# Down projection of one hybrid layer: five groups of eight full products, or two groups of seven half-size forms

## The chip, the core and the metric

The kernel runs on one NeuronCore of one Trainium2 chip. The core has five engines with a queue of their own each: TensorE (PE, with its weight load shown apart as PEld), VectorE (DVE), ScalarE (ACT), GpSimd (POOL) and SyncE (SP), which issues all DMA transfers here. The metric is the device time of one execution in microseconds; the value for a kernel is the median of its runs.

## The reference, cut to what matters

One layer: modulated normalisation, short convolution and bidirectional mLSTM side by side, output projection, then a feed-forward block with a 3-tap convolution between its two projections, and a last normalisation. There are T = 2176 tokens (128 of a prompt, 2048 of a sample), D = 1024 channels and D_FF = 2816 = 22 x 128. All products are in fp32.

```
up = (h2 @ w_up)                          # (T, 2 * D_FF)
up = conv3(up, conv_ffn_w, conv_ffn_b, axis=ffn_axis)
a, gg = jnp.split(up, 2, axis=-1)
x = x + gate2 * ((jax.nn.silu(gg) * a) @ w_down)
...
y_prompt = rmsnorm(xp, final_norm)
y_sample = rmsnorm(xs, final_norm)
```

The change concerns `u @ w_down` with u = silu(gg) * a, that is 2176 x 2816 times 2816 x 1024, and the residual and the normalisation that follow.

## The kernel before, in words

Everything lies in one function, `hymba_kernel`, with channels on the 128 partitions and tokens along the rows. An fp32 product is made of three products in a rounded format: a factor is split into a high half (rounded by ScalarE) and a low half (what is left, by a subtraction), and high x high, high x low and low x high are summed in PSUM. So each operand that TensorE reads has passed ScalarE once and VectorE or GpSimd once.

The kernel has four stages:

1. Phase 0 and 1 (to L543 and on): modulation (`mod_dve`, L505-518), projections of the heads, short convolution, mLSTM, output projection. A generator `side` (L536) is advanced by the loops over the heads and the short convolution; each of its steps adds work that is not of the loop itself: the modulation's rows are multiplied on VectorE from tiles `wm`, five of them in rotation.
2. The up projection (L890-978): already in seven products of half size, in an order `ORDER` that is written out. For each of 22 tiles j of the feed-forward width, its results `raw` go through the convolution `conv` (L893-923: taps on VectorE at L900, ScalarE at L906 and L920, the product at L921), and u is stored to a DRAM tile `uD`.
3. The down projection (L981-1075). Tokens are cut into five groups (L981). For a group, all 22 slices of u are loaded and split (`load_u`, high half L999, low half L1000). For each of eight output blocks m, the 22 x 128 columns of weights are loaded in two halves of 1408 columns, split on ScalarE (L1011), GpSimd and VectorE (L1013, 704 columns each); then 22 x 3 products (L1044-1046) run into one PSUM accumulator `d`. There are four such accumulators. `close` (L1048-1058) takes it out of PSUM with gate and residual in one VectorE operation (L1051) and adds its squares to `ss`. The last product block of the last group is cut at 256 tokens.
4. The last normalisation, `finish` (L1017-1025): PE sums the squares over partitions (`inv_rms`, L124), VectorE and GpSimd make the inverse root (L127, L128), PE spreads it over all partitions (`spread`, L135), VectorE scales the eight blocks (L1024), and each is stored. It is called after the first block of the next group, and at the very end.

The framework puts each engine's instructions into a fixed order beforehand, from the order of the code, and each engine runs its queue in that order; a transfer waits in SP's queue until its buffer is free. The weights of the next block and the u of the next group are asked for in the code ahead of the products that run meanwhile (`nw`, `nus`).

Of the kernel before, what the change touches and what calls it, by code (L numbers as in the profile page):

```python
# [10 lines left out]
F32 = mybir.dt.float32  # L11
# [15 lines left out]
FT = 22  # L27
EPS = 1e-6
# [27 lines left out]
def hymba_kernel(ctx: ExitStack, tc: tile.TileContext, I, O):  # L56
# [17 lines left out]
    uD = dr.tile([FT, P, T], F32, name="uD")  # L74

# [235 lines left out]
    with ExitStack() as ph1:  # L311
# [151 lines left out]
        with tc.tile_pool(name="start", bufs=1, side="right") as stp:  # L463
# [70 lines left out]

            late()
            side = chain(first_stats(), mod_dve())  # L536
# [353 lines left out]
    with ph2:  # L890
        up = ctx.enter_context(tc.tile_pool(name="up", bufs=1))
# [89 lines left out]
    GR = [(0, 436), (436, 436), (872, 436), (1308, 434), (1742, 434)]  # L981
    NG = 436
    with ExitStack() as ph3:
        dq = ph3.enter_context(tc.tile_pool(name="dq", bufs=2, side="right"))
        du = ph3.enter_context(tc.tile_pool(name="du", bufs=8, side="right"))
        pools = {}
        for j0 in range(0, FT, 4):
            pool = ph3.enter_context(tc.tile_pool(name=f"du{j0}", bufs=1))
            for j in range(j0, min(j0 + 4, FT)):
                pools[j] = pool  # L990
        dp = ph3.enter_context(tc.tile_pool(name="dp", bufs=2))
        pd = ph3.enter_context(tc.tile_pool(name="pd", bufs=4, space=PSUM))

        def load_u(j, t0, n):
            f = du.tile([P, NG], F32, name="us")
            Q.dma_start(f[:, :n], uD[j][:, t0:t0 + n])
            uh = pools[j].tile([P, NG], F32R, name=f"uh{j}")
            ul = pools[j].tile([P, NG], F32R, name=f"ul{j}")
            S.activation(uh[:, :n], f[:, :n], AF.Copy)  # L999
            V.tensor_sub(ul[:, :n], f[:, :n], uh[:, :n].bitcast(F32))  # L1000
            return uh, ul

        def load_d(m):
            ws = []
            n = FT * P // 2
            for q in range(2):
                st = dq.tile([P, n], F32, name="st")
                Q.dma_start(st, I["w_down"][m][:, q * n:(q + 1) * n])
                wh = dq.tile([P, n], F32R, name="wh")
                wl = dq.tile([P, n], F32R, name="wl")  # L1010
                S.activation(wh, st, AF.Copy)  # L1011
                for e, a, b in ((G, 0, 704), (V, 704, n)):
                    e.tensor_sub(wl[:, a:b], st[:, a:b], wh[:, a:b].bitcast(F32))  # L1013
                ws.append((wh, wl))
            return ws
# [135 lines left out]
```

## Time and profile before

| | us |
|---|---|
| median of 3 runs | 2602.16 (2601.05 to 2602.48) |
| profiled execution | 2600.9 |
| its span, first to last instruction | 2599.1 |
| phases 0 and 1, to the first up product | about 1100 |
| up projection, to the end of its last product | about 949 |
| down projection, from there to the end of its last product | 539.5 |
| tail, from there to the last transfer | 10.5 |
| TensorE busy in the down projection (536.40 of 539.50) | 99% |

The page's first lines give busy time by engine, and its rows by line (`L1044 PE MATMUL d<-uh,wh`) give the tile written, the tiles read, the shape and the number of instructions. Rows of the timeline have the start in us from the span's beginning, the duration in us, and in brackets the idle time in front and what ended it. A row of the stage table has the stretch, then busy time and count of PE, PEld, DVE, ACT and POOL, the granted TensorE clock, the share of the DMA engines and GB/s. The granted clock over the whole span is 0.990. Rows of one line have minimum / median / maximum in ns, the first and last start, and the shapes. A row of transfers has the count, the KB of one and the us from issue to landing.

### The profile page before, as it was taken

The numbers are of one execution on the slowest core, as the hardware profiler recorded it, in microseconds if no ns is written. First come the engines' busy times: TensorE is split into PE (matmuls) and PEld (weight loads), VectorE is DVE, ScalarE is ACT, GpSimd is POOL, SyncE is SP. The second block draws the span as 40 slices with busy tenths as digits, with TensorE's granted clock in tenths as the row PEclk, the third lists the DMA queues.
The fourth block names the chain that finished last, engine by engine and source line by source line (L and its number), as shares of the span: only waits on it lengthen the run. The fifth ranks groups of instructions, "written<-read, shape, count | busy, mean of one in ns | idle before, by whom it ended". The sixth has DMA issues, their size and how long they took to land.

```text
span 2599.1 us, 40164 instructions
## 1 busy us (share of the span) xinstructions
PE 2520.1 (97%) x15121; PEld 2391.7 (92%) x15121; DVE 1519.6 (58%) x2495; ACT 1091.0 (42%) x1986; POOL 751.5 (29%) x545
## 2 busy tenths in 40 slices
PE   8999999999998989899999999999999999999998
PEld 7999999999998988899999998788888899999998
DVE  3993241223366556787686668867767735535353
ACT  4521152322355445464454446545555524424231
POOL 2442242211334343322121111221221233333332
PEclk9999999999999989999999999999999999999999
DMA  8783142565477877863243224222222647456362
GB/s 278 246 267 92 60 147 85 153 175 163 148 215 242 252 237 222 288 215 126 81 144 124 81 73 143 91 97 82 90 97 82 211 138 239 160 193 224 119 207 84
DMA packets 233380, 414.16 MB, mean 159 GB/s; under 512 B 21586, under 2 KB 173026, under 8 KB 231522
## 3 DMA queue, kind: packets, MB, share of 16 engines
q1 hardware_dynamic: 233186, 411.60, 48.7%
q8 instruction: 119, 1.95, 0.3%
q14 instruction: 75, 0.61, 0.1%
HBM read 316.57 MB, written 94.94 MB: 158 GB/s over the span
## 4 chain that ended last, share of the span: by engine, by line
PE 67%; DMA 6%; DVE 5%; issue 2%; ACT 1%; POOL 1%; SPq 0%; DVEq 0%; POOLq 0%; ACTq 0%
PE d L1044 7%; PE d L1045 7%; PE d L1046 7%; PE pa L955 6%; PE pa L957 6%; PE pa L956 6%; PE acc L203 3%; PE acc L201 3%; PE acc L202 3%; PE pb L955 3%; PE pb L957 3%; PE pb L956 3%; PE pc L956 2%; PE pc L955 2%; PE pc L957 2%
## 5 line engine op out<-in xcount | busy, mean ns | idle before, releaser
L201 PE MATMUL acc<-hH,wh 128*128 128x384 f32 (+1 forms) x1536 | 513.8, 335 | 7.4 <-DVE row L446 4.8
L203 PE MATMUL acc<-hH,wl 128*128 128x384 f32 (+1 forms) x1536 | 506.0, 329 | 0.0
L202 PE MATMUL acc<-hL,wh 128*128 128x384 f32 (+1 forms) x1536 | 505.4, 329 | 0.0
L291 POOL TENSOR_TENSOR wl<-st,wh 128x512 fp32r<-128x512 f32 x132 | 184.1, 1395 | 684.6 <-ACT wh L290 654.8
L110 POOL TENSOR_TENSOR wl<-wst,wh 128x512 fp32r<-128x512 f32 (+1 forms) x160 | 235.7, 1494 | 447.9 <-ACT wh L107 438.3
L955 PE MATMUL pa<-tH,wh 128*128 128x288 f32 (+1 forms) x1056 | 348.2, 330 | 5.8 <-DVE raw L969 3.8
L957 PE MATMUL pa<-tH,wl 128*128 128x288 f32 (+1 forms) x1056 | 346.2, 328 | 1.0 <-DVE wl L291 1.0
L956 PE MATMUL pa<-tL,wh 128*128 128x288 f32 (+1 forms) x1056 | 346.8, 329 | 0.0
L1044 PE MATMUL d<-uh,wh 128*128 128x436 f32 (+3 forms) x902 | 321.8, 357 | 2.4 <-ACT raw L967 2.4
L1045 PE MATMUL d<-ul,wh 128*128 128x436 f32 (+3 forms) x902 | 322.3, 357 | 0.0
L1046 PE MATMUL d<-uh,wl 128*128 128x436 f32 (+3 forms) x902 | 321.2, 356 | 0.0
L201 PEld LDWEIGHTS acc<-hH,wh 128*128 128x128 f32 x1536 | 291.6, 190 | 9.6 <-DVE row L446 5.6
L203 PEld LDWEIGHTS acc<-hH,wl 128*128 128x128 f32 x1536 | 291.4, 190 | 0.2 <-issue 0.2
L202 PEld LDWEIGHTS acc<-hL,wh 128*128 128x128 f32 x1536 | 291.5, 190 | 0.0
L1013 POOL TENSOR_TENSOR wl<-st,wh 128x704 fp32r<-128x704 f32 x80 | 191.1, 2389 | 341.3 <-ACT wh L1011 316.6
L1011 ACT ACTIVATE wh<-st 128x1408 fp32r<-128x1408 f32 x80 | 110.4, 1380 | 330.9 <-PE d L1045 309.5
L900 DVE SCALAR_TENSOR_TENSOR tt<-raw,fw,tt 128x127 f32<-128x127 f32 (+4 forms) x264 | 245.1, 949 | 3.5 <-ACT tt L906 2.5
L955 PEld LDWEIGHTS pa<-tH,wh 128*128 128x128 f32 x1056 | 198.3, 188 | 23.1 <-ACT c L962 2.6
L957 PEld LDWEIGHTS pa<-tH,wl 128*128 128x128 f32 x1056 | 199.0, 188 | 17.0 <-DVE wl L291 1.4
L956 PEld LDWEIGHTS pa<-tL,wh 128*128 128x128 f32 x1056 | 198.7, 188 | 15.5
L290 ACT ACTIVATE wh<-s 128x512 fp32r<-128x512 f32 x176 | 110.9, 630 | 177.0 <-PE pc L956 96.0
L1044 PEld LDWEIGHTS d<-uh,wh 128*128 128x128 f32 x902 | 170.3, 189 | 12.0 <-ACT raw L967 2.8
(215 smaller groups left out, 4892.5 us busy)
## 6 DMA issues: line engine op xcount, KB each, us to landing
st<-in_w_down SPq DMA_DIRECT2D x80, 704.0 KB, 4.1
st<-in_w_up SPq DMA_DIRECT2D x88, 512.0 KB, 4.8
wst<-in_w_in SPq DMA_DIRECT2D x48, 512.0 KB, 4.3
uD<-tt SPq DMA_DIRECT2D x44, 544.0 KB, 2.7
R<-nD SPq DMA_DIRECT2D x34, 512.0 KB, 6.3
wm<-in_w_modr SPq DMA_DIRECT2D x32, 512.0 KB, 4.7
us<-uD SPq DMA_DIRECT2D x66, 218.0 KB, 4.0
wst<-in_w_out SPq DMA_DIRECT2D x24, 512.0 KB, 4.9
```

The costliest lines, as they stand in the source:

```text
L110: G.tensor_sub(wl[:, a:a + n // 2], st[:, a:a + n // 2], wh[:, a:a + n // 2].bitcast(F32))
L201: PE.matmul(acc[:, :n], w_h, hH[:, k, :n], start=(k == 0), stop=False)
L202: PE.matmul(acc[:, :n], w_h, hL[:, k, :n], start=False, stop=False)
L203: PE.matmul(acc[:, :n], w_l, hH[:, k, :n], start=False, stop=(k == KT - 1))
L900: V.scalar_tensor_tensor(o, i, w, o, op0=ALU.mult, op1=ALU.add)
L955: PE.matmul(acc, wh[:, w], rh, start=(kk == 0 and i in (0, 1, 5)), stop=False, skip_group_check=True)
L956: PE.matmul(acc, wh[:, w], rl, start=False, stop=False, skip_group_check=True)
L957: PE.matmul(acc, wl[:, w], rh, start=False, stop=(kk == 3), skip_group_check=True)
L1013: e.tensor_sub(wl[:, a:b], st[:, a:b], wh[:, a:b].bitcast(F32))
L1044: PE.matmul(acc[:, :e - a], wh[:, c], uh[:, a:e], start=(j == 0), stop=False)
L1045: PE.matmul(acc[:, :e - a], wh[:, c], ul[:, a:e], start=False, stop=False)
L1046: PE.matmul(acc[:, :e - a], wl[:, c], uh[:, a:e], start=False, stop=(j == FT - 1))
```

## The change

The down projection is cut in two along the outputs (blocks m and m + 4), along the 22 slices (11 and 11, `KH`), and along pairs of 272 tokens (`NB`). Seven products of half size, each of a sum of weight quarters and a sum of activation quarters, take the place of eight, and the results are combined in SBUF. With weight quarters A11, A12 (output blocks 0 to 3) and A21, A22 (4 to 7), and activation quarters B00, B01, B10, B11 (first index: slices, second: token half), the seven forms are:

| form | weights | activations |
|---|---|---|
| 0 | A11 | B00 |
| 1 | A21 + A22 | B01 - B00 |
| 2 | A21 + A22 - A11 | B11 - B01 + B00 |
| 3 | A22 | B10 - B11 + B01 - B00 |
| 4 | A12 | B10 |
| 5 | A11 - A21 | B11 - B01 |
| 6 | A12 - A21 - A22 + A11 | B11 |

- The four sums of weights are made once, in phase 1, by `down_sums`: eight portions, each of four loads of 704 columns into `wm` tiles, four VectorE operations (L550-553) and four stores to a DRAM tile `wsD` (L556). It is appended to `side`.
- There are two groups of 1088 tokens. Within a group, the loop runs form by form; within a form over eight units (m, p): m of 4 output blocks and p of two token blocks of 544, in the order `SEQ`. A unit is 11 x 3 products of 272 columns (L1137-1139) into one of six accumulators `d`.
- `weights_d` (L1015-1030) loads a form's weights for one m in parts of 768 and 640 columns through two staging tiles `st`; the low half is all VectorE's (L1028), GpSimd has none. `form` (L1042-1062) loads activation quarters and makes the differences on VectorE (L1060) in chunks of 4, 4 and 3 slices, `parts` (L1063-1068) splits them (ScalarE L1066, VectorE L1067). Next form's activations are prepared during the units of this one.
- Forms 0 and 1 are copied out of PSUM by ScalarE into `top` (L1142, L1144); forms 2 to 6 are added by VectorE into `top` and `bot` (L1150-1162). `close` (L1077-1098) then applies gate and residual (L1085) and adds the squares (L1098). `finish` is called for each token half of a block on its own, eight times, three chunks of 128, 128 and 16 tokens each; its scalings (L1108) are taken off a generator, up to four per unit.
- The pool `up` is closed after the last convolution, ahead of the down projection's result tiles.

```diff
+KH = FT // 2
+NB = 272
+    wsD = dr.tile([4, 4, P, KH * P], F32, name="wsD")
...
+            def down_sums():
+                n = KH * P // 2
+                for m in range(4):
+                    for q in range(2):
+                        t = []
+                        for mm, o in ((m + 4, n * 2), (m + 4, 0), (m, 0), (m, n * 2)):
+                            x = stp.tile([P, 1024], F32, name="wm", bufs=5)
+                            Q.dma_start(x[:, :n], I["w_down"][mm][:, o + q * n:o + (q + 1) * n])
+                            t.append(x[:, :n])
+                        yield
+                        a22, a21, a11, a12 = t
+                        V.tensor_add(a22, a21, a22)
+                        V.tensor_sub(a21, a11, a21)
+                        V.tensor_sub(a11, a22, a11)
+                        V.tensor_sub(a12, a12, a11)
+                        yield
+                        for i, x in enumerate((a22, a11, a21, a12)):
+                            Q.dma_start(wsD[i, m][:, q * n:(q + 1) * n], x)
...
-            side = chain(first_stats(), mod_dve())
+            side = chain(first_stats(), mod_dve(), down_sums())
...
-    GR = [(0, 436), (436, 436), (872, 436), (1308, 434), (1742, 434)]
...
+        dw = ph3.enter_context(tc.tile_pool(name="dw", bufs=6, side="right"))
+        db = ph3.enter_context(tc.tile_pool(name="db", bufs=3, side="right"))
+        pd = ph3.enter_context(tc.tile_pool(name="pd", bufs=6, space=PSUM))
+        def weights_d(i, m):
...
+            for a, e in ((0, 6 * P), (6 * P, n)):
+                st = dw.tile([P, 6 * P], F32, name="st", bufs=2)
+                Q.dma_start(st[:, :e - a], w[:, a:e])
+                wh = dw.tile([P, 6 * P], F32R, name="wh")
+                wl = dw.tile([P, 6 * P], F32R, name="wl")
+                S.activation(wh[:, :e - a], st[:, :e - a], AF.Copy)
+                V.tensor_sub(wl[:, :e - a], st[:, :e - a], wh[:, :e - a].bitcast(F32))
...
+        SEQ = ((0, 0), (0, 1), (1, 0), (1, 1), (2, 0), (3, 0), (2, 1), (3, 1))
+        for g in range(2):
+            for i in range(7):
...
+                for k, (m, p) in enumerate(SEQ):
+                    if k in (0, 2, 4):
+                        ws[m + 1] = weights_d(i, m + 1)
...
+                    acc = pd.tile([P, 512], F32, name="d")[:, :NB]
+                    for kk in range(KH):
...
+                        PE.matmul(acc, wh[:, c], uh, start=(kk == 0), stop=False)
+                        PE.matmul(acc, wh[:, c], ul, start=False, stop=False)
+                        PE.matmul(acc, wl[:, c], uh, start=False, stop=(kk == KH - 1))
+                    if i == 0:
+                        outs[m, p] = dp.tile([P, PN], F32, name="top", bufs=10)
+                        S.activation(outs[m, p][:, :NB], acc, AF.Copy)
+                    elif i == 1:
+                        S.activation(outs[m, p][:, NB:], acc, AF.Copy)
+                    else:
...
+                        if i == 2:
+                            V.tensor_add(z, x, acc)
+                            V.tensor_add(y, y, z)
+                        elif i == 3:
+                            V.tensor_add(z, z, acc)
+                        elif i == 4:
+                            V.tensor_add(x, x, acc)
+                            close(g, m, p, 0)
+                        elif i == 5:
+                            V.tensor_add(z, z, acc)
+                            V.tensor_add(v, y, acc)
+                            close(g, m + 4, p, 0, 2)
+                        else:
+                            V.tensor_add(y, y, acc)
+                            close(g, m, p, 1)
```

How the orders move. Outside phase 1 (from the projections of the q heads to the short convolution of the second half of the tokens) and the down projection, each engine has the same instructions in the same order in both kernels. Three places on VectorE follow; a row has the line, the operation, the tile written and the tiles read, and the shape.

VectorE at the end of the modulation and the beginning of the short convolution, before (`y,mt<-wm` and `modT` are the modulation, `cr` and `yr` the short convolution, read from the accumulators `acc`):

```order
L512 SCALAR_TENSOR_TENSOR y,mt<-wm,cB 128x1024 x2
L514 TENSOR_SCALAR modT<-mt,bmod 128x2
L657 MEMSET zc 128x1
L626 COPY mi<-sm_4398 1x4 x2
L388 TENSOR_TENSOR cr<-acc,cr 128x384
L395 SCALAR_TENSOR_TENSOR yr<-cr,scw,yr 128x6x63
L397 SCALAR_TENSOR_TENSOR yr<-cr,scw,yr 128x6x63
L401 TENSOR_TENSOR yr<-acc,yr 128x384
```

The same place after (`wm<-wm` are the weight sums):

```order
L552 TENSOR_TENSOR wm<-wm 128x704
L517 TENSOR_SCALAR modT<-mt,bmod 128x2
L553 TENSOR_TENSOR wm<-wm 128x704
L550 TENSOR_TENSOR wm<-wm 128x704
L551 TENSOR_TENSOR wm<-wm 128x704
L552 TENSOR_TENSOR wm<-wm 128x704
L553 TENSOR_TENSOR wm<-wm 128x704
L391 TENSOR_TENSOR cr<-acc,cr 128x384
L398 SCALAR_TENSOR_TENSOR yr<-cr,scw,yr 128x6x63
L550 TENSOR_TENSOR wm<-wm 128x704
L400 SCALAR_TENSOR_TENSOR yr<-cr,scw,yr 128x6x63
L551 TENSOR_TENSOR wm<-wm 128x704
```

The sums of the first two portions stand between the modulation's last rows and the first `cr`, those of the others between the operations of the short convolution.

VectorE at the passage from the last convolution (`tt`) to the down projection, before (`ul` are low halves of 436 tokens of u):

```order
L969 TENSOR_TENSOR raw_20003<-pc,c_20020 128x512
L1000 TENSOR_TENSOR ul_20235<-us,uh_20234 128x436
L1000 TENSOR_TENSOR ul_20241<-us,uh_20240 128x436
L900 SCALAR_TENSOR_TENSOR tt<-raw_20003,fw,tt 128x1088
L1000 TENSOR_TENSOR ul_20247<-us,uh_20246 128x436
L900 SCALAR_TENSOR_TENSOR tt<-raw_20003,fw,tt 128x1024
L1000 TENSOR_TENSOR ul_20253<-us,uh_20252 128x436
L900 SCALAR_TENSOR_TENSOR tt<-raw_20004,fw,tt 128x1088
L1000 TENSOR_TENSOR ul_20259<-us,uh_20258 128x436
L900 SCALAR_TENSOR_TENSOR tt<-raw_20004,fw,tt 128x1024
```

And after (`wl` are low halves of weights, `bl` those of activations; three `bl` make one token block):

```order
L924 SCALAR_TENSOR_TENSOR tt<-raw_20132,fw,tt 128x1088
L1028 TENSOR_TENSOR wl<-st,wh 128x768
L924 SCALAR_TENSOR_TENSOR tt<-raw_20132,fw,tt 128x1024
L924 SCALAR_TENSOR_TENSOR tt<-raw_20133,fw,tt 128x1088
L1028 TENSOR_TENSOR wl<-st,wh 128x640
L1067 TENSOR_TENSOR bl_20283<-cur_20280,bh_20282 128x1088
L924 SCALAR_TENSOR_TENSOR tt<-raw_20133,fw,tt 128x1024
L1067 TENSOR_TENSOR bl_20289<-cur_20286,bh_20288 128x1088
L1067 TENSOR_TENSOR bl_20295<-cur_20292,bh_20294 128x816
L945 TENSOR_TENSOR tt<-tt 128x1088
L1067 TENSOR_TENSOR bl_20301<-cur_20298,bh_20300 128x1088
```

Where single slices of 436 tokens stood between the taps, chunks of 816 and 1088 columns and the weights' low halves stand now.

VectorE around a norm in the down projection, before (`fr` is the inverse root, `ot` the results):

```order
L1058 TENSOR_TENSOR ss<-ss,sq 128x436
L1013 TENSOR_TENSOR wl<-st,wh 128x704
L1051 SCALAR_TENSOR_TENSOR ot<-d,modT,ot 128x436
L127 TENSOR_SCALAR fr<-st 128x3
L127 TENSOR_SCALAR fr<-st 52x1
L1013 TENSOR_TENSOR wl<-st,wh 128x704
L1024 SCALAR_TENSOR_TENSOR ot<-ot,nrm,st 128x436 x8
```

And after, in form 6 of the first group (`cur` are activation differences, `top` results, `xr` the residual):

```order
L1060 TENSOR_TENSOR cur_22718<-us,cur_22718 128x1088
L1085 SCALAR_TENSOR_TENSOR top<-top,modT,xr 128x272
L1028 TENSOR_TENSOR wl<-st,wh 128x768
L1098 TENSOR_TENSOR ss_22380<-ss_22380,sq 128x272
L1028 TENSOR_TENSOR wl<-st,wh 128x640
L1162 TENSOR_TENSOR top<-top,d 128x272
L130 TENSOR_SCALAR fr<-st 128x2
L1085 SCALAR_TENSOR_TENSOR top<-top,modT,xr 128x272
L130 TENSOR_SCALAR fr<-st 16x1
L1060 TENSOR_TENSOR cur_22765<-us,cur_22765 128x1088
L1098 TENSOR_TENSOR ss_22330<-ss_22330,sq 128x272
L1108 SCALAR_TENSOR_TENSOR top<-top,nrm,st 128x272 x4
```

Between the norm's two steps stood one operation on results, and eight scalings came in one piece; now additions out of PSUM, closings, weights and differences stand around it, and the scalings come in fours.

More of the change, by code (lines that the diff above doesn't have):

```diff
@@ L978, in hymba_kernel @@
                     next(side, None)
[L981 to L982 removed]
+    CK = ((0, 4), (4, 8), (8, KH))
+    PN = 2 * NB
     with ExitStack() as ph3:
[L984 to L1003, printed above, removed]
[L1004 to L1013 removed]
@@ L1086 @@
+        run(after)
 _SHAPES = {"y": (KT, P, T), "s": (P, H, 2, 129), "m": (2, H)}
```

163 lines of the change are left out of this document (103 added, 60 removed).

## The prediction

> **What bounds the kernel now.** I read the page's busy shares first, then the stage table of the down projection, then the timeline of single products there.
>
> ```profile
> span 2599.1 us, 40164 instructions
> PE 2520.1 (97%) x15121; PEld 2391.7 (92%) x15121; DVE 1519.6 (58%) x2495; ACT 1091.0 (42%) x1986; POOL 751.5 (29%) x545
> 2049.10:2068.40 19.30, 16.96 (x77) 15.73 (x78) 16.21 (x22) 12.01 (x20) 1.72 (x1) 0.91 0.86 288
> 2100.00:2400.00 300.00, 300.00 (x1532) 284.10 (x1531) 147.93 (x188) 105.01 (x134) 111.90 (x51) 1.00 0.57 187
> ```
>
> TensorE is busy 97% of the span, and 300.00 of 300 us in the middle of the down projection, where VectorE needs 147.93, DMA has a share of 0.57 and moves 187 GB/s. So the stage costs what its products cost, one behind the other. The spacing of products, by number of columns, is read from pairs of rows whose distance is a known count of products:
>
> ```profile
> 2080.00 0.35 PE L1044 MATMUL d<-uh,wh 128*128 128x436 f32 x1
> 2098.40 0.36 PE L1044 MATMUL d<-uh,wh 128*128 128x436 f32 x1
> 1300.61 0.29 PE L955 MATMUL pa<-tH,wh 128*128 128x288 f32 x1
> 1308.61 0.29 PE L955 MATMUL pa<-tH,wh 128*128 128x288 f32 x1
> 63.49 0.28 PE L348 MATMUL acc<-wh,hL 128*128 128x264 f32 x1
> 65.89 0.28 PE L347 MATMUL acc<-wl,hH 128*128 128x264 f32 x1
> 2587.84 0.27 PE L1045 MATMUL d<-ul,wh 128*128 128x178 f32 x1
> 2588.29 0.27 PE L1046 MATMUL d<-uh,wl 128*128 128x178 f32 x1
> ```
>
> 436 columns: 18.40 us over 93 products, 0.1978. 288 columns: 8.00 over 60, 0.1333. 264 columns: 2.40 over 20, 0.1200. 178 columns: 0.45 over 4, 0.1125, hardly less than 264, so there is a floor near 0.11.
>
> **The products.** Before, the stage has 2706 products: 1584 of 436 columns, 990 of 434, 66 of 256 and 66 of 178. At 0.1978 (scaled by columns down to 256) they make 523.4 us. After, seven forms instead of eight quarter products, each over 8 units of 11 slices by 3 products, twice (two groups of 1088 tokens): 2 x 7 x 8 x 33 = 3696 products of 272 columns. No row has 272; between 264 and 288 lies 0.1200 to 0.1333, a straight line gives 0.1244, and I take 0.125: 3696 x 0.125 = 462.0 us. So 61.4 us are to be had, and the rest of this part is what is paid for it.
>
> In a sentence by itself: the Trainium skill, page "TensorE: Matmul & The Clock Gate", section "Back-to-back issue gap", gives N/2.4 + 2.5 ns for a lone product, which would make 115.8 ns of 272 columns and 428 us of the stage; this trace has 0.1200 at 264 columns where that formula gives 112.5 ns, so the measurement decides.
>
> **The start of the stage.**
>
> ```profile
> 2048.70 0.39 PE L957 MATMUL pa<-tH,wl 128*128 128x512 f32 x1
> 2050.03 1.35 DVE L900 SCALAR_TENSOR_TENSOR tt<-raw,fw,tt 128x1088 f32<-128x1088 f32 x1 [0.37 <-ACT tt L906]
> 2050.81 0.57 ACT L967 ACTIVATE raw<-pa 128x512 f32<-128x512 f32 x1
> 2051.44 0.19 PEld L1044 LDWEIGHTS d<-uh,wh 128*128 128x128 f32 x1 [2.78 <-ACT raw L967]
> 2051.75 1.28 ACT L906 ACTIVATE tt<-raw,fw 128x1088 f32<-128x1088 f32 x1
> 2068.40 0.80 DVE L1051 SCALAR_TENSOR_TENSOR ot<-d,modT,ot 128x128 f32<-128x128 f32 x2 [2.10 <-PE d L1046]
> ```
>
> The last up product ends at 2048.70 + 0.39 = 2049.09, which I call T. The first output's 66 products would take 13.05; its closing starts at T + 19.31. So 6.3 us are lost, 2.35 of them before the first product. After, no product starts before ScalarE has written raw (0.57), a weight half (about 0.7), tt (1.28) and a rounded half of the activations (about 1.1): T + 4.0. VectorE must then make, in one queue, the low halves of both token blocks between taps of 1.35 and 1.28 of the last convolution: by adding up its new order I get the last one for the second block at T + 14.8, and the two first units, ideally 8.25 us, finished at T + 16.4. Loss 8.2. Bounds: 6.3 (as now) to 14.8.
>
> **VectorE's load.**
>
> ```profile
> L1013 DVE TENSOR_TENSOR wl<-st,wh x80: 876/892/2380, 2037.2 to 2572.9; 128x704 fp32r<-128x704 f32 x80
> L1000 DVE TENSOR_TENSOR ul<-us,uh x110: 593/599/2127, 2041.6 to 2485.2; 128x436 fp32r<-128x436 f32 x66, 128x434 fp32r<-128x434 f32 x44
> L921 DVE TENSOR_TENSOR tt<-tt x44: 1276/1286/2379, 1148.5 to 2058.1; 128x1088 f32<-128x1088 f32 x44
> L969 DVE TENSOR_TENSOR raw<-pa,c x66: 440/458/692, 1125.0 to 2045.2; 128x288 f32<-128x288 f32 x44, 128x512 f32<-128x512 f32 x22
> L1024 DVE SCALAR_TENSOR_TENSOR ot<-ot,nrm,st 128x256 f32<-128x256 f32 x8 | 3.2, 477 | 1.6 <-PE st L135 1.6
> 2166.12 0.60 DVE L1058 TENSOR_TENSOR ss<-ss,sq 128x436 f32<-128x436 f32 x1
> L1058 DVE TENSOR_TENSOR ss<-ss,sq x36: 344/2124/2133, 2081.7 to 2589.5; 128x436 f32<-128x436 f32 x21, 128x434 f32<-128x434 f32 x13, 128x256 f32<-128x256 f32 x1, 128x178 f32<-128x178 f32 x1
> ```
>
> 436, 704 and 1088 columns take 0.60, 0.89 and 1.28, so one operation is about 0.16 us and 1.02 ns a column: 272 columns 0.44, 640 0.82, 768 0.95, 816 1.00; read from PSUM, 288 columns take 0.44. Per group of 1088 tokens: 28 weight sets at 0.95 + 0.82, 49.6 (none on GpSimd any more); low halves, 7 x 2 x (1.28 + 1.28 + 1.00), 49.8; differences in forms 1, 2, 3 and 5, 28.5; evacuations and closings 51.1 (7.0, 3.5, 10.1, 19.5 and 11.0 for forms 2 to 6); final scaling, 32 at 0.495, 15.8. Together 195 us against 56 units x 33 x 0.125 = 231 of products: 84%. On the whole that is hidden. It is not in forms 5 and 6, which hold 33.7 + 37.2 = 71 us of VectorE work against 66 of products and 5 of norms in a PE queue that can run ahead by six accumulators: I put 3 us per group on it, 6 in all, and 3 for the change of groups, where ScalarE and VectorE must have all the fresh halves of the second group ready. Bounds 0 and 28: the last row above shows that an addition that takes 0.60 alone took 2.12 in the median, beside GpSimd's weight subtractions, which go away; had one operation in six that price, 71 would become 100. The transfers of a group (weights 20 MB; activations, residuals, results and the rest 32) come to about 52 MB in 235 us, 221 GB/s, under the 288 quoted above.
>
> **The norms.**
>
> ```profile
> 2170.62 1.02 PEld L124 LDWEIGHTS st<-ones,ss 128*128 128x128 f32 x8
> 2171.66 0.19 PEld L1044 LDWEIGHTS d<-uh,wh 128*128 128x128 f32 x1
> 2172.91 1.16 PEld L135 LDWEIGHTS st<-ident,fr 128*128 128x128 f32 x8 [0.16 <-POOL fr L128]
> 2174.12 0.19 PEld L1044 LDWEIGHTS d<-uh,wh 128*128 128x128 f32 x1
> 2172.00 1.57 POOL L128 TENSOR_TENSOR fr<-fr,mhalf 128x3 f32<-128x3 f32 x2 [2.43 <-DVE fr L127]
> ```
>
> A norm takes PE 1.04 + 1.21 = 2.25 us for four chunks of tokens (436), so 1.69 for three (272). Seven stand between products: 11.8. Spreading waits for GpSimd's second power, at its earliest 1.9 us after the sums; the new order puts 10 to 18 products (1.25 to 2.25 us) in between, once only 4. I allow 0.5 for each of the seven: 3.5.
>
> **The end.**
>
> ```profile
> 2590.55 0.22 DVE L127 TENSOR_SCALAR fr<-st 128x1 f32<-128x1 f32 x2 [0.72 <-PE st L124]
> 2592.71 2.57 DVE L1024 SCALAR_TENSOR_TENSOR ot<-ot,nrm,st 128x178 f32<-128x178 f32 x8 [1.95 <-PE st L135]
> ```
>
> The last product ends at 2588.29 + 0.27 = 2588.56, so the stage now takes 539.5 and 10.5 follow to the end. After, the tail has an addition out of PSUM more (0.5), eight scalings at 0.495 instead of 2.57 in all (1.4), and some of the previous norm's scalings ahead of the last evacuation (1.5): 13.9.
>
> **The sums of the weights in phase 1.**
>
> ```profile
> wm<-in_w_modr SPq DMA_DIRECT2D x21, 512.0 KB, 4.1
> 200.00:230.00 30.00, 30.00 (x197) 30.00 (x196) 11.74 (x23) 6.34 (x9) 7.79 (x6) 1.00 0.51 150
> 230.00:263.00 33.00, 33.00 (x214) 33.00 (x213) 8.03 (x12) 6.34 (x9) 7.80 (x6) 1.00 0.21 64
> 232.25 0.56 DVE L388 TENSOR_TENSOR cr<-acc,cr 128x384 f32<-128x384 f32 x1 [6.74 <-PE acc L203]
> 244.86 0.56 DVE L388 TENSOR_TENSOR cr<-acc,cr 128x384 f32<-128x384 f32 x1 [7.89 <-PE acc L203]
> ```
>
> Eight portions of four loads, four subtractions or additions of 704 columns (4 x 0.89 = 3.6 us) and four stores, 2.88 MB or about 10 us at the 288 GB/s seen above. There is room for it in both windows (VectorE 11.74 of 30 and 8.03 of 33, DMA shares 0.51 and 0.21), but VectorE runs in order, and the new order puts two whole portions ahead of the first cr of the short convolution. That cr is then 2 x 13.6 = 27.2 us late, less 5 of loads that land beside the last modulation tiles. Three accumulators are 244.86 - 232.25 = 12.6 us of products, and with four PE stops behind them: 27.2 - 5.0 - 12.6 = 9.6 us. Bounds: 0 (if both portions' transfers overlap) and 25 (if the portions behind the first cr also make PE wait).
>
> **The sum.** Stage: 8.2 + 462.0 + 11.8 + 3.5 + 6 + 3 = 494.5 (now 539.5). Span: 2049.1 + 9.6 + 494.5 + 13.9 = 2567.1. The profiled execution took 2600.9 with a span of 2599.1, so 1.8 lie around it: 2568.9. The median of the runs, 2602.16, is 1.3 above the profiled one: 2570.
>
> **Rivals.**
>
> *Weight staging becomes the bound (slower).* Every form needs weights of its own, 56 sets in halves of 768 and 640 columns, 112 loads where 80 of 1408 were, through two staging buffers, each of which is held from the issue of a load to the end of the subtraction.
>
> ```profile
> st<-in_w_down SPq DMA_DIRECT2D x78, 704.0 KB, 4.1
> L1011 ACT ACTIVATE wh<-st x80: 1362/1381/1387, 2035.8 to 2571.5; 128x1408 fp32r<-128x1408 f32 x80
> ```
>
> Landing 4.1, rounding about half of 1.38 (0.8), subtraction 0.95: 5.85 us, against 8.25 for the two units that a set serves. Each wait in the queues of ScalarE and VectorE, behind an evacuation or a closing that waits for its product, adds to it. At a mean wait of 3.0 us the gain is gone (a cycle of 8.84, 56 x 0.59 = 33); at 4.5 a cycle of 10.3 costs 56 x 2.05 = 115, and the time is 2685. Against it: the three sets of wh and wl let loads run about 12.4 us ahead of their use. Chance 0.07.
>
> *The sums in phase 1 hold PE by their upper bound*, 25 instead of 9.6: 2586. For it speaks that every portion's subtractions stand between the short convolution's in one queue. Chance 0.11.
>
> *VectorE lags in forms 5 and 6 at contended prices*, 28 instead of 6: 2592. Against it speaks that GpSimd hardly works beside it any more. Chance 0.11.
>
> *The narrow products don't deliver*: 272 columns cost like 288, 0.1333. Then 492.7 instead of 462.0, and 2601, no change. Chance 0.05.
>
> *Spacing at the floor* of the 178-column rows, 0.1125: 415.8, 46 less, 2524. In a sentence by itself, this is the side to which the page named above leans. Chance 0.02; the 264-column rows speak against it.
>
> **How the numbers follow.** The forecast case has 0.64 and gives 2570. With its small terms at their lower bounds (sums 0, lag 0, start 6.3, change of groups 0) it is 20.5 lower, 2550, the lower end. Upwards the range takes in both rivals with a small price, 2586 and 2592, with the start at 14.8 in place of 8.2 on some of that: 2597. What is left out is staging, the floor and most of the case without delivery, under 0.2 together with the forecast's tails. A measurement of this kernel tells about 0.2%, 5.2 us, from no change. Faster: 0.64 + 0.02 + 0.11 + most of the lag (0.09) + 0.01 = 0.87. Same: 0.02 of the lag and 0.03 without delivery, 0.05. Slower: staging and 0.01, 0.08.
>
> **What would show it.** Pairs of rows of 272-column products 33 apart should lie 4.1 us apart; the first product near T + 4, and T itself near 2058.7. PE should be busy over 97% from the third unit to the last; forms 5 and 6 should show its only waits, for accumulators freed by VectorE. If PE's idle time is put down to wl or wh of the weights, staging was the bound; if T is beyond 2070, the sums were; if the spacing is not between 0.1233 and 0.127, the main term was mis-sized.

## The result and the profile after

The changed kernel takes 2568.8 us (median of 4 runs, 2567.7 to 2569.9); the kernel before took 2602.3 beside it. The ratio is 0.987, with a 95% interval of 0.985 to 0.989: 33 us less. The forecast was 2570. The profiled execution took 2569.87 with a span of 2568.1; the span forecast was 2567.1.

The page of the changed kernel, its first lines, and then the stage table (stretch, then busy time and count of PE, PEld, DVE, ACT, POOL, granted clock, DMA share, GB/s) for the whole down projection, forms 1 to 3 of the first group (numbered as in the table of forms), its form 5 and its form 6:

```profile
span 2568.1 us, 42559 instructions
...
PE 2469.4 (96%) x16127; PEld 2364.4 (92%) x16127; DVE 1644.1 (64%) x2741; ACT 1112.4 (43%) x2035; POOL 567.0 (22%) x470
```

```profile
2063.70:2555.80 492.10, 481.84 (x3780) 479.15 (x3780) 361.75 (x535) 205.54 (x278) 12.48 (x14) 0.99 0.69 213
2106.70:2206.40 99.70, 99.70 (x795) 99.70 (x794) 61.43 (x75) 38.82 (x51) 0.00 (x0) 1.00 0.66 202
2239.60:2272.80 33.20, 33.20 (x265) 33.20 (x265) 27.01 (x51) 16.11 (x24) 0.00 (x0) 1.00 0.73 225
2272.80:2314.80 42.00, 40.04 (x303) 39.12 (x302) 35.27 (x70) 16.25 (x24) 6.20 (x6) 0.96 0.64 201
```

The down projection takes 492.1 us where it took 539.5, although it has 990 products more; PE never stops in form 5, and form 6, with three norms in it, is 8.8 us longer than the 33.2 of a form without any (the first group's fourth norm falls into form 0 of the second). VectorE works 361.75 us of the 492 (74%; it was 49% in the middle of the stage before), so the margin has shrunk, but it is there.

Two rows of the timeline with a known count between them give the new spacing, and the third is the last product:

```profile
2100.02 0.29 PE L1138 MATMUL d<-bl,wh 128*128 128x272 f32 x1
...
2112.10 0.29 PE L1138 MATMUL d<-bl,wh 128*128 128x272 f32 x1
...
2555.51 0.28 PE L1139 MATMUL d<-bh,wl 128*128 128x272 f32 x1
```

Between the first two lie 96 products: 12.08 / 96 = 0.1258 us. The last product ends at 2555.8, 12.3 us before the span's end.

The passage into the down projection, from the last up product to the first two products of the new kind:

```profile
2063.28 0.40 PE L981 MATMUL pa<-tH,wl 128*128 128x512 f32 x1
2063.75 4.92 SPq L1038 DMA_DIRECT2D cur<-uD  x6
2068.98 1.11 ACT L1066 ACTIVATE bh<-cur 128x1088 fp32r<-128x1088 f32 x1 [1.61 <-DMA cur<-uD]
2070.14 0.60 PE L1137 MATMUL d<-bh,wh 128*128 128x272 f32 x1 [6.47 <-ACT bh L1066]
2071.47 0.59 PE L1138 MATMUL d<-bl,wh 128*128 128x272 f32 x1 [0.73 <-DVE bl L1067]
```

The last up product ends at 2063.7, 14.6 us later than before, because of the sums in phase 1 (below). Then PE waits 6.47 us for activations whose load was issued only at 2063.75. In the first form the clock is low as well; 264 products took 36.6 us there (2070.1 to 2106.7) instead of 33.2:

```profile
2070.10:2076.00 5.90, 5.13 (x21) 4.82 (x22) 5.88 (x6) 5.27 (x6) 0.00 (x0) 0.50 1.05 330
```

What happened in phase 1 shows on VectorE (start, duration, in brackets the wait and what ended it), and in the table of PE's waits (in all, times, longest) from 120 to 300 us:

```profile
203.85 0.88 DVE L553 TENSOR_TENSOR wm<-wm 128x704 f32<-128x704 f32 x1
214.13 0.89 DVE L550 TENSOR_TENSOR wm<-wm 128x704 f32<-128x704 f32 x1 [9.41 <-DMA wm<-in_w_down]
...
217.71 0.55 DVE L391 TENSOR_TENSOR cr<-acc,cr 128x384 f32<-128x384 f32 x1
...
224.89 0.89 DVE L550 TENSOR_TENSOR wm<-wm 128x704 f32<-128x704 f32 x1 [5.24 <-DMA wm<-in_w_down]
```

```profile
PE acc L204 <- DVE cr L391: 9.0, 2, 8.1
PE acc L204 <- DVE yr L404: 5.1, 2, 3.8
```

The first cr starts at 217.71; before it was 204.95. VectorE stood 9.41 us in front of the second portion's load with a cr behind it that was ready, and again 5.24 us in front of the third. PE, its accumulators full, waited 8.1 and 3.8 us, and behind each wait it ran a stretch at half clock (last section). The stretch from 200 to 230 us after, where 197 products had run:

```profile
200.00:230.00 30.00, 18.04 (x93) 17.40 (x92) 13.74 (x19) 1.85 (x4) 1.09 (x1) 0.82 0.85 302
```

What the sums cost is read from one product ahead of this place and one behind it. They are the 1201st and the 2001st matmul in PE's order, the same two in every kernel; here they are before (L201, L203) and after (L204, L206):

```profile
179.62 0.34 PE L201 MATMUL acc<-hH,wh 128*128 128x384 f32 x1
...
306.13 0.34 PE L203 MATMUL acc<-hH,wl 128*128 128x384 f32 x1
```

```profile
178.24 0.34 PE L204 MATMUL acc<-hH,wh 128*128 128x384 f32 x1
...
324.29 0.34 PE L206 MATMUL acc<-hH,wl 128*128 128x384 f32 x1
```

They lie 126.51 us apart before and 146.05 after, so 19.5 us are lost between them. T is only 14.6 later, because this execution was 1.4 us ahead at the first of the two and gained 3.6 between the second and T. The experiments show that these parts vary from kernel to kernel by several us.

### The profile page after: what moved, and what is told of

Same layout as the page of the kernel before. It is cut to its first block, busy times and chain, and to the rows that moved or that the text cites. A ratio compares the mean times of both kernels' runs of the same rounds, so it can differ in the third digit from the quotient of the medians.

```text
span 2568.1 us, 42559 instructions
## 1 busy us (share of the span) xinstructions
PE 2469.4 (96%) x16127; PEld 2364.4 (92%) x16127; DVE 1644.1 (64%) x2741; ACT 1112.4 (43%) x2035; POOL 567.0 (22%) x470
## 4 chain that ended last, share of the span: by engine, by line
PE 64%; DMA 6%; DVE 5%; issue 2%; ACT 2%; POOL 1%; SPq 0%; DVEq 0%; ACTq 0%; POOLq 0%
PE pa L979 6%; PE pa L981 6%; PE pa L980 6%; PE d L1138 5%; PE d L1139 5%; PE d L1137 5%; PE acc L204 4%; PE acc L206 4%; PE acc L205 4%; PE pb L979 3%; PE pb L981 3%; PE pb L980 3%; PE pc L979 2%; PE pc L980 2%; PE pc L981 2%
## 5 line engine op out<-in xcount | busy, mean ns | idle before, releaser
L204 PE MATMUL acc<-hH,wh 128*128 128x384 f32 (+1 forms) x1536 | 515.8, 336 | 23.3 <-DVE cr L391 9.9
L206 PE MATMUL acc<-hH,wl 128*128 128x384 f32 (+1 forms) x1536 | 506.5, 330 | 0.0
L1137 PE MATMUL d<-bh,wh 128*128 128x272 f32 x1232 | 357.3, 290 | 6.5 <-ACT bh L1066 6.5
L1138 PE MATMUL d<-bl,wh 128*128 128x272 f32 x1232 | 357.6, 290 | 0.7 <-DVE bl L1067 0.7
L1139 PE MATMUL d<-bh,wl 128*128 128x272 f32 x1232 | 357.8, 290 | 0.0
L204 PEld LDWEIGHTS acc<-hH,wh 128*128 128x128 f32 x1536 | 292.6, 191 | 26.6 <-DVE cr L391 11.0
L206 PEld LDWEIGHTS acc<-hH,wl 128*128 128x128 f32 x1536 | 292.2, 190 | 0.2 <-issue 0.2
L1137 PEld LDWEIGHTS d<-bh,wh 128*128 128x128 f32 x1232 | 233.4, 190 | 7.0 <-ACT bh L1066 6.9
L1138 PEld LDWEIGHTS d<-bl,wh 128*128 128x128 f32 x1232 | 233.6, 190 | 1.2 <-DVE bl L1067 1.0
L1139 PEld LDWEIGHTS d<-bh,wl 128*128 128x128 f32 x1232 | 233.5, 190 | 0.0
```

The source lines that it names most:

```text
L204: PE.matmul(acc[:, :n], w_h, hH[:, k, :n], start=(k == 0), stop=False)
L206: PE.matmul(acc[:, :n], w_l, hH[:, k, :n], start=False, stop=(k == KT - 1))
L1137: PE.matmul(acc, wh[:, c], uh, start=(kk == 0), stop=False)
L1138: PE.matmul(acc, wh[:, c], ul, start=False, stop=False)
L1139: PE.matmul(acc, wl[:, c], uh, start=False, stop=(kk == KH - 1))
```

## The experiments

In this table T is the end of the last up product; "first" is the first down product after T, "stage" runs from T to the end of the last product, "tail" from there to the end of the span. They come from one profiled execution of each; the medians and the ratios to the kernel before come from the timed runs.

| kernel | T | first | stage | tail | span | median, ratio to before |
|---|---|---|---|---|---|---|
| before | 2049.1 | 2.4 | 539.5 | 10.5 | 2599.1 | 2602.3 |
| changed | 2063.7 | 6.5 | 492.1 | 12.3 | 2568.1 | 2568.8, 0.987 [0.985, 0.989] |
| e1 no sums | 2047.6 | 5.3 | 491.3 | 13.5 | 2552.4 | 2546.9, 0.979 [0.977, 0.982] |
| e2 sums paced | 2046.5 | 5.2 | 490.6 | 13.3 | 2550.4 | 2550.4, 0.980 [0.978, 0.982] |
| e3 half on GpSimd | 2065.2 | 6.5 | 497.4 | 13.0 | 2575.6 | 2576.4, 0.991 [0.988, 0.993] |
| e4 nine slices | 2069.6 | 5.6 | 425.2 | 13.4 | 2508.2 | 2510.7, one run |
| e5 one staging tile | 2057.6 | 5.2 | 647.8 | 12.9 | 2718.2 | 2720.1, one run |
| e6 norms apart | 2064.0 | 5.3 | 490.0 | 17.4 | 2571.4 | 2570.6, 0.988 [0.986, 0.990] |
| e7 activations early | 2060.1 | 7.0 | 497.1 | 13.3 | 2570.5 | 2571.9, 0.988 [0.986, 0.991] |
| e8 e2, e6 and e7 | 2049.1 | 7.0 | 493.2 | 17.4 | 2559.7 | 2557.0, 0.983 [0.981, 0.985] |

**e1, the sums left out.**

```diff
-            side = chain(first_stats(), mod_dve(), down_sums())
+            side = chain(first_stats(), mod_dve())
...
+            w = I["w_down"][m + 4 * (i % 2)][:, (i // 4) * n:(i // 4 + 1) * n]
```

> The weight sums of phase 1 are left out, loads and stores with them; the forms that use them take plain quarters of the weights instead, so the work of the down projection is the same in size and its results are not the layer's. Theory (the sums hold PE at the short convolution): the end of the last up product goes from 2063.7 back to within 1 us of the kernel before (2049.1), nothing else changes, and the time falls by 14.6 us, to about 2554. Rival (only the waits of 14.1 us that the profile puts on cr and yr are the sums', or PE makes up for them later and the rest of the delay is from elsewhere): the last up product ends at 2055 or later and the time falls by less than 9.

T is 2047.6, 16.1 us under the changed kernel, and the stage is as long as there (491.3). The stretch 190 to 290 us of the kernel before, the changed one, e1 and e2 (next), in this order:

```profile
190.00:290.00 100.00, 100.00 (x641) 100.00 (x640) 34.77 (x60) 20.06 (x30) 23.15 (x17) 1.00 0.28 87
```

```profile
190.00:290.00 100.00, 85.82 (x512) 84.56 (x511) 53.27 (x75) 14.81 (x23) 21.29 (x14) 0.93 0.84 294
```

```profile
190.00:290.00 100.00, 100.00 (x643) 100.00 (x642) 34.49 (x58) 19.57 (x29) 24.38 (x18) 1.00 0.26 84
```

```profile
190.00:290.00 100.00, 99.38 (x633) 99.06 (x632) 63.22 (x92) 18.63 (x28) 24.08 (x16) 1.00 0.84 284
```

129 products fewer fit into these 100 us with the sums than before, and all are back without them. Between the two products named above, e1 takes as long as the kernel before (0.0 us more), so the loss of 19.5 us there is all the sums'; the rival is out. The theory's size was too small: the time fell by 20 to 22 us (by the ratios and by the medians) and not by 14.6, which fits the 19.5 at the place and not the 14.6 of T. (The profiled execution, at 2554.3, was the slowest of the four; the others took 2546.5 to 2547.2.)

**e2, the sums paced.**

```diff
+                        gate.append(rq.tile([P, 1], F32, name="one", bufs=12))
+                        V.tensor_scalar(gate[-1], yr[:, :1], 0.0, 1.0, op0=ALU.mult, op1=ALU.add)
...
-                        V.tensor_add(a22, a21, a22)
+                        V.scalar_tensor_tensor(a22, a21, gate[2 * m + q], a22, op0=ALU.mult, op1=ALU.add)
```

> The sums stay in phase 1, but the first operation of portion k is multiplied by a 1.0 that is made from the result of unit k of the short convolution, so the order can't put it ahead of that unit: one portion behind each of the first eight units instead of two ahead of the first. Theory (VectorE, in order, stood in front of two portions' transfers while PE had only four accumulators): no wait of PE for cr or yr is left between 190 and 330 us, the last up product ends between 2048 and 2053, and the time is 11 to 15 us under the changed kernel, 2554 to 2558. Rival (the 23 MB of transfers themselves are in the way, wherever VectorE waits for them): the last up product still ends at 2058 or later, and the gain is under 6.

T is 2046.5 and no wait for cr or yr is left. The rows of VectorE show the sums behind the short convolution's operations instead of ahead of them:

```profile
204.66 0.55 DVE L391 TENSOR_TENSOR cr<-acc,cr 128x384 f32<-128x384 f32 x1
...
208.14 0.95 DVE L553 SCALAR_TENSOR_TENSOR wm<-wm,one 128x704 f32<-128x704 f32 x1
...
213.00 0.56 DVE L391 TENSOR_TENSOR cr<-acc,cr 128x384 f32<-128x384 f32 x1 [1.13 <-PE acc L206]
```

DMA moves 284 GB/s in that stretch where the changed kernel moved 294, and PE is busy 99.38 of 100 us. So the bytes were not in the way, and the sums cost 0.9 us between the two products, instead of 19.5, when they stand in the right place. The theory holds, but both of its figures were missed on the fast side: T by 1.5 us, and the time by 3.6 (18.4 under the changed kernel and not 11 to 15), because the sums had cost more than T showed. At 2550.4 this is the fastest kernel with the whole computation, 2.0% under the kernel before.

**e3, half of the weights' low halves on GpSimd.**

```diff
-                V.tensor_sub(wl[:, :e - a], st[:, :e - a], wh[:, :e - a].bitcast(F32))
+                for eng, b0, b1 in ((G, 0, (e - a) // 2), (V, (e - a) // 2, e - a)):
+                    eng.tensor_sub(wl[:, b0:b1], st[:, b0:b1], wh[:, b0:b1].bitcast(F32))
```

> GpSimd makes half of each low half of the down projection's weights again, VectorE the other half; all else as in the changed kernel. Theory (VectorE is not the bound of any form, only TensorE's stream is): the time stays within 3 us of the changed kernel, though single VectorE operations stretch while GpSimd works beside them. Rival (VectorE's margin in forms 4 to 6 is small enough that stretched operations hold PE): 10 to 28 us slower, with PE waiting for weights or for an accumulator in the forms 4 to 6. Third possibility (VectorE was late and the 47 us taken off it help): 3 us faster or more.

The stage became 5.3 us longer. Nearly all of it lies in form 6 of the first group, with its three norms: 47.1 us instead of 42.0. Forms 1 to 5 take 33.2 each in both groups, as in the changed kernel. The table of PE's waits from T on:

```profile
PE st L138 <- POOL fr L131: 7.8, 4, 5.0
PE d L1138 <- ACT bh L1067: 6.5, 1, 6.5
PE st L127 <- DVE ss L1099: 2.4, 1, 2.4
PE d L1139 <- DVE bl L1068: 2.3, 1, 2.3
```

The wait of 5.0 us is put down to GpSimd's inverse root, but GpSimd had itself waited for VectorE's step of it (L130):

```profile
2293.76 0.15 DVE L130 TENSOR_SCALAR fr<-st 128x2 f32<-128x2 f32 x1
...
2293.99 1.46 POOL L131 TENSOR_TENSOR fr<-fr,mhalf 128x2 f32<-128x2 f32 x2 [3.67 <-DVE fr L130]
```

PE's sums had ended at 2288.49. Seven operations stood between in VectorE's queue, two of them stretched by 1.1 us in all, so most of this wait is the new order and not the stretching. No wait for weights or accumulators appears. So the theory's core stands, since outside the norms and the start VectorE holds nothing, but the time is 8 to 10 us longer (by the medians and by the ratios) where 3 were allowed; the rival's 10 to 28 us are just missed. The time itself decides little: the interval touches that of the changed kernel. What taking work off VectorE brought is more telling, groups of the down projection by shape, first e3, then the changed kernel:

```profile
L1086 DVE SCALAR_TENSOR_TENSOR top<-top,modT,xr 128x272 f32<-128x272 f32 x27 | 18.2, 674 | 0.3
...
L1152 DVE TENSOR_TENSOR top<-top,bot 128x272 f32<-128x272 f32 x16 | 9.7, 608 | 0.4
...
L1151 DVE TENSOR_TENSOR bot<-top,d 128x272 f32<-128x272 f32 x16 | 6.9, 434 | 7.3 <-PE d L1140 7.3
```

```profile
L1085 DVE SCALAR_TENSOR_TENSOR top<-top,modT,xr 128x272 f32<-128x272 f32 x28 | 13.9, 498 | 0.3
...
L1151 DVE TENSOR_TENSOR top<-top,bot 128x272 f32<-128x272 f32 x16 | 7.0, 440 | 0.4
L1150 DVE TENSOR_TENSOR bot<-top,d 128x272 f32<-128x272 f32 x16 | 7.0, 434 | 9.9 <-PE d L1139 9.7
```

Half of the weights' subtractions left VectorE, and its busy time did not fall (367.9 us in the 498 from 2065 to 2563, against 361.75): operations with two operands in SBUF grew from 498 to 674 ns and from 440 to 608 in the mean, while the one that reads an accumulator stayed at 434. The growth is in those that ran while GpSimd worked: of the 27 in L1086, 18 did, with a mean of 763 ns (489 to 1151), and the other 9 took 497 (486 to 502). The Trainium skill, page "GPSIMD Engine Reference", section "Specifications", says that GpSimd shares its SBUF interfaces with VectorE and contends with operations that have two SBUF inputs; these rows agree.

**e4, nine of eleven slices.**

```diff
-                    for kk in range(KH):
+                    for kk in range(KH - 2):
...
-                        PE.matmul(acc, wl[:, c], uh, start=False, stop=(kk == KH - 1))
+                        PE.matmul(acc, wl[:, c], uh, start=False, stop=(kk == KH - 3))
```

> Two of the eleven slices of every unit are left out, 672 products in all, so the results are not the layer's; loads, splits, sums, evacuations and norms stay. Theory (TensorE's stream sets the stage, the others have margin): 672 x 0.1258 = 84.5 us less, 2484, or up to 20 more, 2505, where DMA is already at 306 GB/s (form 4) and VectorE at 81 to 85% (forms 5 and 6). Rival (a set of weights cycles through staging in nearly the 8.3 us of its two units, so staging is as tight as TensorE): the cycle can't shrink, less than 25 us gained, 2544 or more.

The stage fell by 66.9 us, to 425.2, of the 84.5 that the products make up; the time was 2510.7, 6 above the theory's range, with a T that was 5.9 us later than in the changed kernel although the edit touches nothing ahead of it, so about 2505 at an equal T. PE's waits in the stage:

```profile
PE st L138 <- POOL fr L131: 6.3, 4, 2.3
PE d L1137 <- ACT bh L1066: 5.6, 1, 5.6
PE d L1138 <- DVE bl L1067: 4.6, 3, 3.5
PE d L1139 <- DVE wl L1028: 4.3, 6, 1.5
```

At 27 products a unit the halves of activations and weights begin to hold PE, by a few us each. The staging rival (less than 25 us gained) is out: most sets of weights now cycle in 6.8 us. At an equal T the upper end of the theory's range is met. So of 84.5 us of products taken off (17% of the stage) 66.9 (14%) are gained, and the rest goes to the other engines and the norms. From which point on they hold PE was not tried.

**e5, one staging tile.**

```diff
-                st = dw.tile([P, 6 * P], F32, name="st", bufs=2)
+                st = dw.tile([P, 6 * P], F32, name="st", bufs=1)
```

> One staging tile for the down projection's weights instead of two; all else as in the changed kernel. If the chain load, rounding, subtraction of each part is what a staging tile is held for (3.6 + 0.8 + 0.9 = 5.3 us by the medians), the two parts of a set follow each other: 10.6 us a set against 8.3 for its two units, 56 sets x 2.3 = 129 us slower, about 2698; with the queue waits of ScalarE and VectorE added (2 us a part) 350 slower. If the next load overlaps the chain's end in some way or is not tied to it, less than 30 us slower.

The stage became 155.7 us longer, 2.8 us for each of 56 sets: a set cycles in 8.3 + 2.8 = 11.1 us in the mean, 0.5 above the bare chain of 10.6. The time, 2720.1 in one run, is 22 above the 2698 of the bare chain. PE waits for each set:

```profile
PE d L1137 <- ACT wh L1027: 76.7, 55, 3.1
PE d L1139 <- DVE wl L1028: 16.1, 33, 1.5
```

These waits are 92.8 of the 155.7 us; the granted clock of the stage was 0.92, where it was 0.99 in the changed kernel, and how the rest divides is not worked out. So the prediction's slower rival is a real mechanism, and the chain of load, rounding and subtraction sets its size. That it would need a wait of some 3 us per part with two tiles stays the prediction's estimate; no run shows it.

**e6, a unit between a norm's two steps.**

```diff
-        def finish(g, p, half, outs, ss):
+        def finish(g, p, half, outs, ss, gap=4):
...
             inv_rms(ss, NB, r)
+            for _ in range(gap):
+                yield
             rb = spread(r, NB)
...
-                    after = chain(after, finish(g, 1, 1, dict(outs), ss.pop((1, 1))))
+                    after = chain(after, finish(g, 1, 1, dict(outs), ss.pop((1, 1)), 4 * (1 - g)))
```

> One unit of 33 products (4.15 us) stands between a norm's sums and its spreading in six of the eight norms, where 4 to 18 products stood; the last two, whose scalings make the tail, are left as they were. In the changed kernel the norms took 16.9 us out of the stream of products, 7 x 1.53 = 10.7 of it their own matmuls. Theory (PE waits there for GpSimd's powers and for the sums of squares): the waits for the powers (4.0 us) go, the stage is 4 to 6 us shorter. Rival (the wait goes to the sums of squares, 2.4 us and more, or VectorE's scalings come later and hold an accumulator): less than 2 us.

The stage is 2.1 us shorter, 1.2 of it at the start and not at the norms; the tail is 5 longer. The theory's 4 to 6 us are missed. The gain is about the rival's, but in the stage not by the rival's mechanism. Form 6 of the two groups became 5.5 and 2.1 us shorter (36.5 and 36.6), as the theory said; then the last norm of the first group lost 6.2, in form 0 of the second (42.4 instead of 36.2). There PE waited for GpSimd's powers again, and restarted at half clock. The row shows two operations of 2 columns and 1 column in 5.25 us:

```profile
2338.77 5.25 POOL L131 TENSOR_TENSOR fr<-fr,mhalf 128x2 f32<-128x2 f32 x2 [15.23 <-DVE fr L130]
```

The median of such an operation in this kernel is 0.77. In the tail, the seventh norm's scalings now stand ahead of the last norm's sums (PE waits 3.5 us for a scaling). Why the power took so long, with VectorE at subtractions meanwhile, wasn't tried.

**e7, memory for the first activations.**

```diff
+        dc = ph3.enter_context(tc.tile_pool(name="dc", bufs=1, side="right"))
         dw = ph3.enter_context(tc.tile_pool(name="dw", bufs=6, side="right"))
...
-                cur[p, c] = fetch(db.tile([P, (CK[c][1] - CK[c][0]) * NB], F32, name=f"cur{p}{c}", bufs=1),
+                cur[p, c] = fetch(dc.tile([P, (CK[c][1] - CK[c][0]) * NB], F32, name=f"cur{p}{c}", bufs=1),
```

> The tiles of the first activation quarters are given the memory that the up projection leaves first, ahead of the weights' tiles; their loads then stand ahead of the weights' in SyncE's queue. Theory (the first product waited 6.5 us because the memory of these tiles was free only with the last up product, so that a load of 5.1 us began then): it starts 4 to 4.6 us after the last up product and the span behind that falls by 2. Rival (the weights, now loaded later, take the place of the activations): the first product starts 6 us after it or later, and nothing is gained.

The first product came 7.0 us after T. The activations were there, and ScalarE rounded all six pieces at one go. The weights' tiles had moved into the late memory, so that their load was issued at T; and their rounding stands behind the six pieces in ScalarE's queue:

```profile
2060.20 0.82 SPq L1025 DMA_DIRECT2D st<-in_w_down  x2
```

```profile
2060.66 5.64 ACT L1067 ACTIVATE bh<-cur 128x1088 fp32r<-128x1088 f32 x6
2066.21 1.46 ACT L1028 ACTIVATE wh<-st 128x768 fp32r<-128x768 f32 x2
```

The weights' first load had landed 3.3 us after its issue, at 2063.5, but ScalarE was at the activations from 2060.66 to 2066.3 without a pause and rounded the weights only then. So the rival's time came, by its mechanism only in part: the last 2.7 us of the wait are ScalarE's order and not the memory. The theory's first half is right: in both kernels the operand in the memory that the up projection's last product holds is loaded from T on. The stage is 5.0 us longer than in the changed kernel, 1.7 of it at the start and 3.2 at the norms of the first group (form 6 43.6 instead of 42.0, the next form 37.7 instead of 36.2); why the norms took longer wasn't tried.

**e8, the three together.** Its edits are those of e2, e6 and e7.

> The three edits together: sums paced by the short convolution, norms with a unit between their two steps, activations in memory that is free early. They touch different places, so the gains should add up: 13 + 5 + 2 = 20 us under the changed kernel, 2549. If one of them fails by its own rival, 2552 to 2562.

2557.0: T at 2049.1 is e2's part; the start of 7.0 is e7's and the tail of 17.4 e6's. The parts add up, with two of them losses. By the medians e2 alone is 6 us shorter; the intervals of the two ratios touch.

## Why the prediction was right, point by point

| term | predicted | measured |
|---|---|---|
| products, 3696 | 462.0 (0.125) | 465.0 (0.1258) |
| start of the stage | 8.2 | 9.8 (6.5 ahead of the first product, 3.3 in the first form) |
| seven norms between products | 15.3 (11.8 and 3.5) | 16.9 |
| lag in forms 5 and 6 | 6 | 0 |
| change of groups | 3 | 0 |
| stage | 494.5 | 492.1 |
| tail | 13.9 | 12.3 |
| delay of T by the sums | 9.6 | 14.6 (19.5 lost at the sums, 5.0 gained elsewhere) |
| span | 2567.1 | 2568.1 |

- **Products.** The main term was right to 0.7%, and by the mechanism that was forecast; 0.1258 lies in the stated 0.1233 to 0.127, and no two products of the stage start less than 0.119 apart. By the formula for a lone product in the Trainium skill, page "TensorE: Matmul & The Clock Gate", section "Back-to-back issue gap", an estimate for this width is 0.1158; the measured stream is 9% slower.
- **Start.** The sum of the loss was nearly right, its account was not. The prediction put ScalarE's four operations at T + 4.0 and VectorE's queue behind. The step that it left out is memory: the activations' tiles lie where the up projection's last operands lay, so that the load is issued at T and takes 5.1 us. And the clock was at 0.50 for the first 6 us of products.
- **Norms.** 16.9 is the sum of all distances above one spacing between 2285 and 2552; 7 x 1.53 = 10.7 is the matmuls' own part. Of the other 6.2, three waits for GpSimd's powers make up 2.9, and a stretch of 3.4 us at clock 0.50 behind the first norm (2291.1 to 2294.5) about 1.7.
- **VectorE's lag and the change of groups** were paid for and not used: no row shows the waits for accumulators that the prediction expected in forms 5 and 6. Adding up durations overstates VectorE's need. The durations of its rows in the stage do add up to 390, as reckoned, but neighbouring rows overlap, and its busy time is 361.75. In form 5 it is 27.0 us (30.9 by durations) where 33.7 were reckoned, in part because a closing of 544 columns takes 0.78 and not two of 0.495.
- **The sums** went the way that was written: two portions ahead of the first cr, VectorE in front of their loads, PE with full accumulators. The size was off by a factor of two: 19.5 us at the place instead of 9.6. The first cr was 12.8 late and not 22, but it found PE already waiting for 8.1, so the cover was some 5 us and not 12.6; the next portions added waits of 3.8 and of about 1, and PE ran at half clock behind two of the waits (last section). In all six kernels with the same order the two products of phase 1 lie 18.3 to 20.4 us further apart than before, without the sums or with the paced ones 0.0 to 0.9 us. So this term is steady. T varies much more among the same six kernels, from 2057.6 to 2069.6, by what happens ahead of the first of the two products and behind the second; e2, which has no delay to make up, also gains 4.5 us there. That T came out only 14.6 late was luck.
- **The errors** of the terms are +3.0 (products), +1.6 (start), +1.6 (norms) and +5.0 (T) on one side and -9 (lag, change of groups) and -1.6 (tail) on the other: 0.6 in all, and 0.4 of the stage left over. The +5.0 of T is itself about +10 of the sums and -5 of other parts. So the forecast came within 1 us by cancelling; its single terms were off by up to 10.
- **Rivals.** Staging holds PE with one tile (e5), and other engines hold it in part with two slices fewer (e4); neither showed in the changed kernel. The spacing of 0.1258 rules out both rivals about the products. The sums' rival (25 us) is the one that came nearest to what happened.

## What to carry to other kernels

A product form with fewer and narrower products is worth its count times the spacing measured at the new width, as long as the other engines keep up (here VectorE was busy for 27.0 of 33.2 us in a form in which PE never stopped); read that spacing from the trace of any stage that has a near width. Side work on an engine that runs in order must be ordered by when its data can be there, not by when the engine has room: the same 23 MB and 32 operations cost 19.5 us ahead of the short convolution's operations and 0.9 behind them. Such a cost is read between two instructions on either side of the place; the end of a long stage moves by other things too. A first load can begin no earlier than its memory is free, so the passage between two stages is read from what last used the memory of each first operand, and then from the order in which the engines take the operands up (e7).

## What the runs showed of the hardware

- After a wait of 8.1 us PE restarted at half clock: its products of 384 columns in the changed kernel's phase 1, first soon after the wait, then 4 us later, go 0.32 us apart and then 0.17, and the granted clock from 200 to 230 us was 0.82:

```profile
219.44 0.52 PE L204 MATMUL acc<-hH,wh 128*128 128x384 f32 x1
219.76 0.52 PE L205 MATMUL acc<-hL,wh 128*128 128x384 f32 x1
...
223.51 0.33 PE L204 MATMUL acc<-hH,wh 128*128 128x384 f32 x1
223.68 0.33 PE L205 MATMUL acc<-hL,wh 128*128 128x384 f32 x1
```

The same is seen behind the wait of 6.5 us at the start of the stage (0.50 from 2070.1 to 2076.0). Behind the wait of 3.8 us PE ran at full clock for 0.8 us and then at half for 3.4 (229.4 to 232.8, products of 256 columns 0.21 apart instead of 0.12). Half of each of these stretches is lost, an estimate of 1.7 to 3 us on top of each of the three waits.
- Work given from VectorE to GpSimd came back in full as longer VectorE operations. Those with two operands in SBUF grew while GpSimd worked (e3: means 498 to 674 and 440 to 608 ns); the one with an operand in PSUM stayed at 434.
- GpSimd's power on 1 or 2 columns took 0.54 to 4.7 us (e6); the cause is open.
